# Earlier first tiles and a re-ordered output projection in a hybrid S5/Conformer step

## The chip, the cores and the metric

The kernel runs on one core of one Trainium2 chip. The core has a matrix engine (TensorE, PE in the profile, with its weight loads counted apart as PEld), a vector engine (VectorE, DVE), a scalar engine (ScalarE, ACT), a general engine (GpSimd, POOL) and a queue engine that here only issues transfers (SyncE, SP). 16 DMA engines move data. The metric is the device time of one execution in microseconds (us); less is better. The time before is 1400.62 us, the median of three runs from 1399.85 to 1401.19 us.

## The reference

One decoder layer is computed for 1024 prompt tokens and 8 sample tokens (1032 columns in all), model width 1024, in float32:

```python
xn = rmsnorm(x, g_mix);  z = xn @ w_in              # 1024 -> 3584
u, cv, cg = z[:, :512], z[:, 512:1024], z[:, 1024:1536]
gates = sigmoid(z[:, 1536:])                        # 2 x 1024
y, hr, hi = s5_layer(u, ...)                        # complex state scan, 32 groups x 64 states
yg = gelu(y) @ w_glu;  ya = yg[:, :1024] * sigmoid(yg[:, 1024:])
c = silu(layernorm(causal_dwconv(cv * sigmoid(cg))))   # 31 taps
yb = c @ w_pw
merged = gates[:, :1024] * ya + gates[:, 1024:] * yb
x = x + merged @ w_out
hn = rmsnorm(x, g_ffn) @ w_ff_in                    # 1024 -> 2 x 2816
x = x + (silu(hn[:, :2816]) * hn[:, 2816:]) @ w_ff_out
return rmsnorm(x, g_final), new states
```

## The kernel before, in words

Activations lie transposed: model channels on the 128 partitions, the 1032 tokens along the free axis. A product of float32 quality is made of three float16 products: each weight tile and each activation tile is split into a high half and a low half, and `mtile` (L584) or `mcol` (L1116) adds high x high, high x low and low x high in PSUM. So that the halves stay in range, every weight tile is first scaled by a power of two. `wload` (L565) is that chain for one 128-column slice of weights: `wdma` (L479) brings it as float32 into a tile `wr` (three buffers); `wscale` (L526) takes the sum of squares with one ScalarE instruction in `sumsq` (L513), then the maximum over partitions with GpSimd's partition_all_reduce in `spread` (L518), then two short VectorE steps in `pow2` (L497, L498); `wsplit16` (L556) writes the high half on ScalarE (L558) and the low half on VectorE (L562) into the tiles `wh` and `wl` (three buffers each). The squares themselves are of no use and are written into the tile that will later take the high half (`his[i].bitcast(BF16)`).

The stages are, in order: norm and transposes of the nine x tiles (`load_x`, `norm`, `xpose`, L647 to L723) together with the u columns of w_in (`u_chunk`, L733) and the parameters of the S5 branch (`prep`); the S5 scan (L839 on), with the convolution input `conv_in` and gate products as other work for TensorE; `glu` and the convolution; the pointwise product `pw` (L1092); the output projection `out` (L1132) with its weights `wout` (L1124); the FFN blocks (`ff_in` L1184, then w_ff_out); the final norm.

An identity matrix `ident` is needed for every transpose on TensorE. It is made by `make_identity` (L628), which ends in one GpSimd instruction, an affine select.

Around w_out: `residual(m)` (L1074) loads 128 channels of x again, transposes them in three PSUM tiles of pool `ms` (two banks, shared with other short uses) and copies them to `x1[m]` on ScalarE. All merged activations are then scaled by one number (`ascale`, from the maximum of `mss`) and split into `mh` for three token chunks. `out(c)` multiplies chunk c in groups of three, three and two columns of tiles, each group in a three-bank PSUM tile of pool `mm` (two such tiles), and adds the product, scaled by `io`, to `x1[m]` (L1143). `io` is made by one instruction (`invs`, L508) from `so`, which holds the scales of all eight w_out tiles.

The order of the work on each engine isn't written by hand. A planner simulates the program and takes, on each engine, the ready instruction of the highest priority; the priority is the place in the program, moved forward by 3000 places inside `hp()` and by 20000 inside `wscale`. On the chip each engine and each transfer queue then works strictly in the order fixed by the planner, and an instruction that waits holds up what is behind it. Tiles with a tag share a fixed number of buffers, and a tile waits until the last user of its buffer is done.

Of the kernel before, what the change touches and what calls it, by code (L numbers as in the profile page):

```python
# [9 lines left out]
F32 = mybir.dt.float32  # L10
# [8 lines left out]
P = 128  # L19
D = 1024  # L20
# [16 lines left out]
class S5:  # L37
# [400 lines left out]
def hybrid_step(ctx: ExitStack, tc: tile.TileContext, x_prompt, x_sample, state_ssm_re, state_ssm_im,  # L438
# [34 lines left out]
    def hp():  # L473
        return tc.high_priority(offset=HPO)
# [50 lines left out]

    def wscale(raws, his, o=None):  # L526
# [10 lines left out]
    def wscale_pe(raws, his):  # L537
        with tc.high_priority(offset=HPS):
            ss = cp.tile([P, 2], F32, name=nm("uss"), tag="uss", bufs=2)
            pt = pst.tile([P, 512], F32, name=nm("pws"), tag="pu")  # L540
            for i, raw in enumerate(raws):
                sumsq(raw, his[i].bitcast(BF16), ss[:, i:i + 1])
                T.matmul(pt[:, 0:1], ones, ss[:, i:i + 1], start=(i == 0), stop=(i == len(raws) - 1))
# [21 lines left out]
    def wload(src, r0, kt, c0):  # L565
        raw = wdma(src, r0, kt, c0)
        hi, lo = (wp.tile([P, kt, P], F16, name=nm(t), tag=t) for t in ("wh", "wl"))
        s = wscale([raw], [hi])
        return wsplit16(raw, hi, lo, s), s

    def wload2(src, cs, dst=None, o=None):
# [4 lines left out]
        h, l = dst or (wp.tile([P, 2, 4, P], F16, name=nm(t), tag=t) for t in ("wh", "wl"))  # L576
        s = wscale([raw], [h], o)
        wsplit16(raw, h, l, s)
# [93 lines left out]
    for r0, src, n in ((0, g_ffn, 8), (8, conv_b, 4), (12, conv_ln_g, 4), (16, conv_ln_b, 4)):  # L672
        GP.dma_start(gw[r0:r0 + n], src[0].rearrange("(r p) -> r p", p=P))
    pt = ms.tile([P, 512], F32, name="pgv", tag="ms")
# [83 lines left out]
    pairs = [wpair(), wpair()]  # L758
    wus = [wscale_pe(raw, [p[0] for p in pairs])]
# [314 lines left out]
    def residual(m):  # L1074
        xc = sb("xc", (P, 8, P))
        SY.dma_start(xc, x_prompt[0][:, m * P:(m + 1) * P].rearrange("(j k) d -> j k d", k=8))
        xcs = cp.tile([8, P], F32, name=nm("xcs"), tag="xcs", bufs=2)
        SY.dma_start(xcs, xsm[:, m * P:(m + 1) * P])
        x1[m] = xT = sa("x1")
        for q in range(3):  # L1080
            pt = ms.tile([P, 512], F32, name=nm("pxt"), tag="ms")
            if q < 2:
                for i in range(4):
                    T.transpose(pt[:, i * P:(i + 1) * P], xc[:, 4 * q + i], ident)
                A.copy(xT[:, 512 * q:512 * q + 512], pt)
            else:
                T.transpose(pt[:, :8], xcs, ident[:8, :8])
                A.copy(xT[:, D:], pt[:, :8])

# [42 lines left out]
    def out(c):  # L1132
# [48 lines left out]
    for c in range(3):  # L1181
        out(c)

    def ff_in(n, ss):  # L1184
        if n == 0:
            ws = [wload(w_ff_in, 0, 8, c0) for c0 in (0, DFF)]
            inv = [invs(s, gsc[:, 2:3]) for _, s in ws]
            pts = [mpsum() for _ in range(2)]
            for cs in ((0, 1), (2,)):
                for q in range(2):  # L1190
                    for c in cs:
                        a, b = B3[c], B3[c + 1]
                        mcol(ws[q][0], [(h[:, a:b], l[:, a:b]) for h, l in xg], pts[q][:, c, :b - a])
            g1, s1 = sa("g1"), sb("s1")
            with hp():
                for d, z, (a, b) in ((0, slice(0, 2), (0, 768)), (1, 2, (768, TOK))):
                    v = [t[:, a:b] if d else t[:, a:b].rearrange("p (c n) -> p c n", c=2) for t in (s1, g1)]
                    n_ = (b - a) if d else 384
                    A.activation(v[0], pts[0][:, z, :n_], AF.Sigmoid, scale=inv[0])
# [28 lines left out]
    def wlast(i):  # L1228
# [107 lines left out]
```

## Time and profile before

| what | value |
|---|---|
| median of 3 runs | 1400.62 us |
| profiled execution, its own time | 1400.05 us |
| its span in the trace | 1398.3 us |
| TensorE busy | 1303.8 us, 93% of the span |
| VectorE busy | 800.6 us, 57% |
| ScalarE busy | 535.3 us, 38% |
| GpSimd busy | 98.9 us, 7% |
| mean transfer rate | 69 GB/s |

TensorE is busy for all but 94.5 us of the span. The shares are means: between 710 and 1346 us, in the FFN, TensorE is busy without a break, while the idle time lies at the start, in the S5 stage, around w_out and at the end. A busy TensorE may also run at a lower granted clock (PEclk in the views of stretches, 1.00 is full speed).

### The profile page before, as it was taken

What the parts mean: (1) busy time and instruction counts of PE and PEld (TensorE: products, weight loads), DVE (VectorE), ACT (ScalarE), POOL (GpSimd) and SP (SyncE); (2) the same over time, 40 slices, a digit from 0 to 9 for tenths busy, and PEclk for the clock granted to TensorE, in tenths of its full rate; (3) what the DMA queues carried; (4) which work ended last, traced back from release to release, by engine and by line L of the source; (5) the groups of instructions that cost most, each with busy time, mean ns of one, the idle gap of its engine ahead of it and who ended that gap; (6) DMA issues with size and microseconds to landing.
All of it is one profiled execution on the core that took longest, in us unless ns stands there. A gap on an engine that the chain in (4) does not pass through costs nothing.

```text
span 1398.3 us, 22132 instructions
## 1 busy us (share of the span) xinstructions
PE 1303.8 (93%) x8877; PEld 892.6 (64%) x8877; DVE 800.6 (57%) x1830; ACT 535.3 (38%) x882; POOL 98.9 (7%) x208
## 2 busy tenths in 40 slices
PE   3898798999998999599989999999999999999996
PEld 2776565666665666367656666666666666666665
DVE  5976888989996635646532433335432434342547
ACT  5834333453334434822332422324232422342412
POOL 5000001100010000000000000000000000000100
PEclk9999899999998999799999999999999999999999
DMA  7445754341121115320011112111221112110103
GB/s 191 126 96 119 141 109 107 99 115 37 55 63 45 31 57 145 117 61 1 1 50 51 29 54 76 46 41 32 65 62 54 29 54 76 46 49 27 50 27 122
DMA packets 168976, 96.45 MB, mean 69 GB/s; under 512 B 12799, under 2 KB 165003, under 8 KB 168873
## 3 DMA queue, kind: packets, MB, share of 16 engines
q1 hardware_dynamic: 167469, 92.44, 24.3%
q0 software_dynamic: 896, 1.63, 0.6%
q8 instruction: 69, 1.13, 0.3%
q10 hardware_dynamic: 507, 0.97, 0.3%
q14 instruction: 35, 0.28, 0.1%
HBM read 76.72 MB, written 9.65 MB: 62 GB/s over the span
## 4 chain that ended last, share of the span: by engine, by line
PE 70%; DVE 14%; issue 9%; DMA 3%; ACT 1%; POOL 1%; SPq 1%; DVEq 0%; ACTq 0%; POOLq 0%
PE mm L591 57%; PE mm L1120 7%; DVE acc L895 3%; PE pfo L1278 2%; PE pu L731 2%; DVE wl L562 2%; DMA Y<-X 1%; DVE tb L895 1%; POOL sv L518 1%; DMA U<-ud 1%; DVE mg L968 1%; DMA M<-kvd 1%; DVE mg L965 0%; DVE xgt L1156 0%; PE ptr L721 0%
## 5 line engine op out<-in xcount | busy, mean ns | idle before, releaser
L591 PEld LDWEIGHTS <-wh 128*128 128x128 f16 x4656 | 457.5, 98 | 234.2 <-issue 5.4
L591 PE MATMUL mm<-xgp,wh 128*128 128x344 f16 x2016 | 350.6, 310 | 4.5 <-DVE py L497 4.5
L591 PEld LDWEIGHTS <-wl 128*128 128x128 f16 x2328 | 228.8, 98 | 112.3 <-issue 0.8
L513 ACT ACTIVATE wh<-wr 128x1024 bf16<-128x1024 f32 (+2 forms) x114 | 109.1, 957 | 407.0 <-PE mm L591 264.4
L591 PE MATMUL mm<-xn,wh 128*128 128x344 f16 (+2 forms) x1152 | 205.6, 313 | 1.9 <-ACT ut L743 1.1
L591 PE MATMUL mm<-xgp,wl 128*128 128x344 f16 x1008 | 202.7, 310 | 0.0
L562 DVE SCALAR_TENSOR_TENSOR wl<-wr,wsc,wh 128x1024 f16<-128x1024 f32 (+2 forms) x112 | 129.8, 1160 | 63.7 <-ACT wh L558 61.2
L558 ACT ACTIVATE wh<-wr,wsc 128x1024 f16<-128x1024 f32 (+2 forms) x112 | 117.0, 1045 | 116.5 <-DVE wsc L498 109.4
L591 PE MATMUL mm<-hp,wh 128*128 128x344 f16 x912 | 157.8, 309 | 0.0
L518 POOL PARTITION_ALL_REDUCE sv<-wss x124 | 67.1, 541 | 1088.6 <-ACT wh L513 1038.8
L523 DVE TENSOR_SCALAR sv<-sv 128x1 f32<-128x1 f32 x124 | 18.9, 152 | 180.7 <-POOL sv L518 180.7
L591 PE MATMUL mm<-xn,wl 128*128 128x344 f16 (+2 forms) x576 | 118.7, 313 | 0.0
L1210 DVE SCALAR_TENSOR_TENSOR g<-mm,inv,g 128x1032 f32<-128x1032 f32 x21 | 27.2, 1293 | 127.2 <-PE mm L591 127.2
L1120 PE MATMUL mm<-mh,wo 128*128 128x384 f16 (+1 forms) x576 | 90.3, 319 | 3.9 <-DVE x L1143 2.8
L591 PE MATMUL mm<-hp,wl 128*128 128x344 f16 x456 | 91.3, 309 | 0.0
L1261 DVE SCALAR_TENSOR_TENSOR x<-mm,inv,x 128x1032 f32<-128x1032 f32 x32 | 41.3, 1292 | 72.3 <-PE mm L591 72.3
L1120 PEld LDWEIGHTS <-wo 128*128 128x128 f16 x576 | 57.7, 101 | 35.3 <-issue 8.9
L591 PE MATMUL mm<-gyp,wh 128*128 128x344 f16 x384 | 66.6, 309 | 1.4 <-DVE mg L968 0.8
L895 DVE SCALAR_TENSOR_TENSOR acc<-t,cws,acc 128x511 f32<-128x511 f32 (+14 forms) x60 | 44.9, 749 | 0.0
L895 DVE SCALAR_TENSOR_TENSOR acc<-c,cw,acc 128x511 f32<-128x511 f32 (+14 forms) x60 | 43.6, 746 | 0.0
L591 PE MATMUL mm<-gyp,wl 128*128 128x344 f16 x192 | 38.4, 309 | 0.0
L1278 PE MATMUL pfo<-hp,wlp 128*128 128x392 f16 (+2 forms) x216 | 34.1, 309 | 0.0
(379 smaller groups left out, 1401.5 us busy)
## 6 DMA issues: line engine op xcount, KB each, us to landing
wr<-in_w_ff_in_dram SPq DMA_DIRECT2D x44, 512.0 KB
wr<-in_w_in_dram SPq DMA_DIRECT2D x28, 512.0 KB
wr<-in_w_ff_out_dram SPq DMA_DIRECT2D x24, 320.0 KB
xt<-in_x_prompt_dram SPq DMA_DIRECT2D x8, 512.0 KB
cosi<-pc SPq DMA_DIRECT2D x32, 128.0 KB
wr<-in_w_glu_dram SPq DMA_DIRECT2D x16, 256.0 KB
wr<-in_w_out_dram SPq DMA_DIRECT2D x8, 512.0 KB
xc<-in_x_prompt_dram SPq DMA_DIRECT2D x8, 512.0 KB
```

Source lines behind the costliest of these rows:

```text
L513: A.activation(junk, src, AF.Square, accum_out=o)
L518: GP.partition_all_reduce(v, ss, P, RMAX)
L523: V.tensor_scalar(v, v, 1e-28, None, MAXI)
L558: A.mul(hi, raw, s)
L562: V.scalar_tensor_tensor(lo[:, sl], raw[:, sl], s, hi[:, sl], MUL, SUB)
L591: T.matmul(pt[:, c, :b - a], ww[:, k], aa[:, a:b], start=(k == 0 and i == 0), stop=(k == n - 1 and i == 2))
L731: T.matmul(o, ww[:, k], aa[:, c0:c0 + w], start=(k == 0 and i == 0), stop=(k == 7 and i == 2))
L895: V.scalar_tensor_tensor(o[:, q:], x[:, 0:HT - q], w[q], o[:, q:], MUL, ADD)
L1120: T.matmul(o, w[a][:, k], acts[k][b], start=(k == 0 and i == 0), stop=(k == n - 1 and i == 2))
L1210: V.scalar_tensor_tensor(c3(g1), z, inv, c3(g1), MUL, MUL)
L1261: V.scalar_tensor_tensor(c3(x1[m]), z, inv, c3(x1[m]), MUL, ADD)
L1278: T.matmul(pt[:, :w], wl[m][a][:, k], hid[k][b][:, c0:c0 + w], start=(k == 0 and i == 0), stop=(k == nb - 1 and i == 2))
```

## The change

The change has four parts. The shortened diff:

```diff
-            dma.dma_start(t[64:128], t[0:64])
+            dma.dma_start(t[64:128], b[0].rearrange("g p c -> p g c"))
...
+    wjunk = cp.tile([P, D], BF16, name="wjunk")
-                sumsq(raw, his[i].bitcast(BF16), ss[:, i:i + 1])
+                sumsq(raw, jview(raw), ss[:, i:i + 1])
...
-    make_identity(nc, ident)
     GP.memset(zi[:, P:], 0.0)
-    GP.memset(ones, 1.0)
+    V.memset(ones, 1.0)
+    V.tensor_tensor_scan(jr, ones, ones, 0.0, MUL, ADD)
+    pj = ms.tile([P, 512], F32, name="pj", tag="ms")
+    T.matmul(pj[:, 0:1], jr[0:1, :], ones[0:1, 0:1], start=True, stop=True)
+    V.tensor_copy(jc, pj[:, 0:1])
+    V.tensor_scalar(ident, jr, jc, None, ALU.is_equal)
...
     s5.load_a(GP)
+    raw = [wdma(w_in, 0, 8, P * m) for m in range(2)]
     with hp():
         load_x(2)
-    raw = [wdma(w_in, 0, 8, P * m) for m in range(2)]
-    for k in range(3, NX):
-        load_x(k)
-    s5.load_b(GP)
+        load_x(3)
+    raw.append(wdma(w_in, 0, 8, 2 * P))
+    with hp():
+        for k in range(4, 9):
+            load_x(k)
+        s5.load_b(SY)
-    GP.dma_start(cwn, conv_w[0])
+    SY.dma_start(cwn, conv_w[0])
...
     def residual(m):
-        xc = sb("xc", (P, 8, P))
-        SY.dma_start(xc, ...)
+        with hp():
+            v = sb("xc", (P, 8, P))
+            SY.dma_start(v, ...)
-        for q in range(3):
-            pt = ms.tile([P, 512], F32, name=nm("pxt"), tag="ms")
...
+        pt = mpsum()
+        for q in range(2):
+            for i in range(4):
+                T.transpose(pt[:, q, i * P:(i + 1) * P], xc[q][:, i], ident)
+        T.transpose(pt[:, 2, :8], xcs, ident[:8, :8])
+        A.copy(xT[:, :512], pt[:, 0])
+        V.tensor_copy(xT[:, 512:D], pt[:, 1])
+        V.tensor_copy(xT[:, D:], pt[:, 2, :8])
...
         for gr in G3:                      # in out(c)
+            if c == 0:
+                for m in gr:
+                    if m >= 4:
+                        residual(m)
...
-    for m in range(3):
+    for m in range(6):
         wout(m)
     for m in range(4):
         residual(m)
...
-        for c in range(3):                 # all three chunks split under hp()
+    def msplit(c):                         # one chunk; hp() for chunk 0 only
+    msplit(0)
-    for m in range(3, 8):
+    for m in range(6, 8):
         wout(m)
-        if m < 7:
-            residual(m + 1)
     io = invs(so, mcx, "io", 1)
     for c in range(3):
+        if c < 2:
+            msplit(c + 1)
         out(c)
...
     def ff_in(n, ss):                      # n == 0
-        # products of chunks 0, 1 and of chunk 2 for both halves, then all gating under hp()
+        # products of chunks 0, 1, their gating at the priority of wscale; then chunk 2 likewise
```

First, the identity is made on VectorE (a running sum gives 1 to 128 along a row, one product on TensorE gives the same numbers down the partitions, one comparison gives the matrix). Second, the x tiles 2 to 8 are issued with high priority, and the S5 parameters of `load_b`, the convolution weights and the small vectors go through SP's queue instead of GpSimd's; both halves of B now come from HBM. Third, the squares of `wscale` and `wscale_pe` go to one scratch tile `wjunk`. Fourth, around w_out, six instead of three `wout` come ahead, residuals 4 to 7 move into `out(0)`, a residual uses one tile of pool `mm` and copies on two engines, the splits of chunks 1 and 2 come in between, and the gating of the first FFN tile is placed between its products.

More of the change, by code (lines that the diff above doesn't have):

```diff
@@ L6 @@
 from concourse import mybir
-from concourse.masks import make_identity
 from concourse._compat import with_exitstack
@@ L524, in spread, with jview, wscale @@
         return v
-    def wscale(raws, his, o=None):
+    wjunk = cp.tile([P, D], BF16, name="wjunk")
+    def jview(raw):
+        sh = list(raw.shape)[1:]
+        n = 1
+        for d in sh:
+            n *= d
+        j = wjunk[:, :n]
+        if len(sh) == 2:
+            return j.rearrange("p (a b) -> p a b", a=sh[0])
+        return j.rearrange("p (a b c) -> p a b c", a=sh[0], b=sh[1])
+    def wscale(raws, o=None):
         with tc.high_priority(offset=HPS):
@@ L535, in wscale, with wscale_pe @@
         return o
-    def wscale_pe(raws, his):
+    def wscale_pe(raws):
         with tc.high_priority(offset=HPS):
@@ L541, in wscale_pe @@
             for i, raw in enumerate(raws):
-                sumsq(raw, his[i].bitcast(BF16), ss[:, i:i + 1])
+                sumsq(raw, jview(raw), ss[:, i:i + 1])
                 T.matmul(pt[:, 0:1], ones, ss[:, i:i + 1], start=(i == 0), stop=(i == len(raws) - 1))
@@ L567, in wload @@
         hi, lo = (wp.tile([P, kt, P], F16, name=nm(t), tag=t) for t in ("wh", "wl"))
-        s = wscale([raw], [hi])
+        s = wscale([raw])
         return wsplit16(raw, hi, lo, s), s
@@ L576, in wload2 @@
         h, l = dst or (wp.tile([P, 2, 4, P], F16, name=nm(t), tag=t) for t in ("wh", "wl"))
-        s = wscale([raw], [h], o)
+        s = wscale([raw], o)
         wsplit16(raw, h, l, s)
@@ L627, in hybrid_step @@
     ident = zi[:, :P]
-    make_identity(nc, ident)
     GP.memset(zi[:, P:], 0.0)
     ones = cp.tile([P, P], F32, name="ones")
-    GP.memset(ones, 1.0)
+    V.memset(ones, 1.0)
+    jr = cp.tile([P, P], F32, name="jr")
+    V.tensor_tensor_scan(jr, ones, ones, 0.0, MUL, ADD)
+    pj = ms.tile([P, 512], F32, name="pj", tag="ms")
+    T.matmul(pj[:, 0:1], jr[0:1, :], ones[0:1, 0:1], start=True, stop=True)
+    jc = cp.tile([P, 1], F32, name="jc")
+    V.tensor_copy(jc, pj[:, 0:1])
+    V.tensor_scalar(ident, jr, jc, None, ALU.is_equal)
     e5, e5c, e5t, est = ExitStack(), ExitStack(), ExitStack(), ExitStack()
@@ L663, in hybrid_step @@
     s5.load_a(GP)
+    raw = [wdma(w_in, 0, 8, P * m) for m in range(2)]
     with hp():
         load_x(2)
-    raw = [wdma(w_in, 0, 8, P * m) for m in range(2)]
-    for k in range(3, NX):
-        load_x(k)
-    s5.load_b(GP)
+        load_x(3)
[4 more added lines that the diff above has]
+        s5.load_b(SY)
     cwn = kp.tile([CW, 512], F32, name="cwn", tag="Q", bufs=2)
-    GP.dma_start(cwn, conv_w[0])
+    SY.dma_start(cwn, conv_w[0])
     for r0, src, n in ((0, g_ffn, 8), (8, conv_b, 4), (12, conv_ln_g, 4), (16, conv_ln_b, 4)):
-        GP.dma_start(gw[r0:r0 + n], src[0].rearrange("(r p) -> r p", p=P))
+        SY.dma_start(gw[r0:r0 + n], src[0].rearrange("(r p) -> r p", p=P))
     pt = ms.tile([P, 512], F32, name="pgv", tag="ms")
@@ L758, in hybrid_step @@
     pairs = [wpair(), wpair()]
-    wus = [wscale_pe(raw, [p[0] for p in pairs])]
+    wus = [wscale_pe(raw[:2])]
     wui = [invs(wus[0], gxc[:, 1:2], "uinv", 2)]
@@ L763, in hybrid_step @@
     wu.append(wsplit16(raw[1], *pairs[1], wus[0], parts=4))
-    raw += [wdma(w_in, 0, 8, P * m) for m in range(2, 4)]
-    for k in range(NX, 9):
-        load_x(k)
+    raw.append(wdma(w_in, 0, 8, 3 * P))
     norm(groups[1])
@@ L769, in hybrid_step @@
     pairs = [[kt_(t, bufs=2) for _ in range(2)] for t in ("cosi", "M")]
-    wus.append(wscale_pe(raw[2:4], [p[0] for p in pairs]))
+    wus.append(wscale_pe(raw[2:4]))
     wui.append(invs(wus[1], gxc[:, 1:2], "uinv", 2))
@@ L1074, in residual @@
     def residual(m):
-        xc = sb("xc", (P, 8, P))
-        SY.dma_start(xc, x_prompt[0][:, m * P:(m + 1) * P].rearrange("(j k) d -> j k d", k=8))
+        with hp():
+            v = sb("xc", (P, 8, P))
+            SY.dma_start(v, x_prompt[0][:, m * P:(m + 1) * P].rearrange("(j k) d -> j k d", k=8))
+        xc = [v[:, 0:4], v[:, 4:8]]
         xcs = cp.tile([8, P], F32, name=nm("xcs"), tag="xcs", bufs=2)
@@ L1079, in residual @@
         x1[m] = xT = sa("x1")
-        for q in range(3):
-            pt = ms.tile([P, 512], F32, name=nm("pxt"), tag="ms")
[L1082 to L1088, printed above, removed]
+        pt = mpsum()
[6 more added lines that the diff above has]
+        V.tensor_copy(xT[:, D:], pt[:, 2, :8])
     wpw, mss = [], cp.tile([P, 8], F32, name="mss")
@@ L1126, in wout @@
         t = pair(sa("wo", (P, 2, 8, P), F16))
-        s = wscale([raw], [t[0]], so[:, m:m + 1])
+        s = wscale([raw], so[:, m:m + 1])
         wo.append(wsplit16(raw, t[0], t[1], s))
@@ L1170, in hybrid_step @@
         msc, mcx = ascale(mss, "msc")
-        for c in range(3):
+    def msplit(c):
+        with tc.high_priority(offset=HPO if c == 0 else 0):
             for m in range(8):
@@ L1188, in ff_in @@
             pts = [mpsum() for _ in range(2)]
-            for cs in ((0, 1), (2,)):
+            g1, s1 = sa("g1"), sb("s1")
+            for z, c0, c1 in ((slice(0, 2), 0, 2), (2, 2, 3)):
                 for q in range(2):
-                    for c in cs:
+                    for c in range(c0, c1):
                         a, b = B3[c], B3[c + 1]
                         mcol(ws[q][0], [(h[:, a:b], l[:, a:b]) for h, l in xg], pts[q][:, c, :b - a])
[L1194 to L1198, printed above, removed]
+                a, b = B3[c0], B3[c1]
+                n_ = 384 if c0 == 0 else b - a
+                v = [t[:, a:b].rearrange("p (c n) -> p c n", c=2) if c0 == 0 else t[:, a:b] for t in (s1, g1)]
+                with tc.high_priority(offset=HPS):
                     A.activation(v[0], pts[0][:, z, :n_], AF.Sigmoid, scale=inv[0])
@@ L1233, in wlast @@
         h, l = pair(sa("wlp", (P, 2, nb, 2 * P), F16))
-        s = wscale([raw], [h], swl[:, i:i + 1])
+        s = wscale([raw], swl[:, i:i + 1])
         wsplit16(raw, h, l, s)
@@ L1302 @@
 NA = 21
-NX = 5
 GA = 5
```

## The prediction

> **What bounds the kernel now.** I read the page, then a table of stretches, then the timeline at the stretches where TensorE (PE) isn't full. Columns of the table: stretch, its length, busy us of PE, PEld, DVE, ACT, POOL, then PE's granted clock, DMA share, GB/s.
>
> ```profile
> span 1398.3 us, 22132 instructions
> 0.00:14.00 14.00, 0.02 (x1) 0.02 (x1) 0.27 (x1) 4.73 (x7) 1.90 (x10) 1.00 0.92 257
> 14.00:18.00 4.00, 1.35 (x5) 1.16 (x5) 3.22 (x28) 2.19 (x4) 3.99 (x6) 1.00 0.63 228
> 18.00:24.00 6.00, 4.43 (x16) 2.76 (x16) 5.61 (x38) 3.33 (x7) 6.00 (x8) 1.00 0.55 117
> 24.00:34.00 10.00, 6.26 (x39) 5.26 (x38) 9.95 (x49) 7.47 (x15) 6.70 (x19) 1.00 0.50 125
> 34.00:54.00 20.00, 15.07 (x115) 11.93 (x115) 18.81 (x97) 17.59 (x34) 0.97 (x2) 0.91 0.54 169
> 54.00:84.00 30.00, 29.80 (x260) 25.77 (x261) 28.07 (x104) 17.55 (x34) 0.00 (x0) 1.00 0.23 63
> 240.00:437.00 197.00, 191.42 (x1297) 128.28 (x1294) 185.78 (x338) 83.36 (x111) 20.50 (x23) 0.99 0.26 72
> 553.90:626.70 72.80, 56.83 (x322) 34.37 (x321) 39.18 (x84) 42.26 (x82) 3.21 (x9) 0.88 0.35 102
> 704.00:710.00 6.00, 6.00 (x28) 3.30 (x26) 2.71 (x5) 2.20 (x3) 0.00 (x0) 0.61 0.31 91
> 710.00:1346.00 636.00, 636.00 (x4364) 426.74 (x4362) 246.62 (x492) 214.18 (x310) 31.33 (x80) 1.00 0.17 50
> ```
>
> From 710 to 1346 PE is busy in every microsecond at full clock: nothing in the change shortens that, however soon weights are ready. The same holds nearly for 240 to 437. The change can gain in three places: 0 to 54 (PE idle 14 + 2.65 + 1.57 + 3.74 + 4.93 = 26.9), around w_out (554 to 627) and at the entry of the FFN (699 to 710).
>
> **Part 1, identity and first transfers.** Timeline of the start:
>
> ```profile
> 4.89 1.06 ACT L702 ACTIVATE junk<-xt 128x1024 bf16<-128x1024 f32 x1 [2.24 <-DMA xt<-in_x_prompt_dram]
> 13.64 0.28 POOL masks.py:199 TENSOR_SCALAR_AFFINE_SELECT zi<-zi 128x128 f32<-128x128 f32 x1 [11.44 <-issue]
> 14.29 0.17 DVE L677 COPY gt<-pgv 128x8 f32<-128x8 f32 x1 [10.88 <-PE pgv L675]
> 17.41 0.75 DVE L707 TENSOR_SCALAR xt<-xt,ry 128x1024 f32<-128x1024 f32 x1
> 26.89 0.15 PEld L731 LDWEIGHTS <-wh 128*128 128x128 f16 x1
> 28.84 3.27 SPq L482 DMA_DIRECT2D wr<-in_w_in_dram  x2
> 34.30 1.06 ACT L513 ACTIVATE wu<-wr 128x1024 bf16<-128x1024 f32 x1 [2.79 <-DMA wr<-in_w_in_dram]
> masks.py:199 POOLq MODIFY_POOL_CONFIG  x2: 37/37/37, 2.3 to 2.3; - x2
> 93.09 1.03 PE L591 MATMUL mm<-xn,wh 128*128 128x344 f16 x6 [1.12 <-ACT ut L743]
> L518 POOLq MODIFY_POOL_CONFIG  x2: 1/1/1, 31.2 to 31.3; - x2
> 38.15 0.38 POOL L518 PARTITION_ALL_REDUCE sv<-wss  x1 [7.11 <-ACT wh L513]
> L371 DVE TENSOR_TENSOR_SCAN Y<-mag,X x32: 393/398/424, 121.9 to 245.8; 128x128 f32<-128x128 f32 x32
> ```
>
> GpSimd changes its configuration at 2.3 us and reaches the affine select only at 13.64; until then PE and DVE stand still, though the first x tile was squared at 4.89. The new identity needs a memset, a scan (0.40, the L371 row), one small product with its hand-overs (0.37, which lies between the end of the affine select and the copy at 14.29), a copy (0.17, as L677) and a 128x128 comparison (no row; between that 0.17 and the 0.75 of eight times its size, L707, I take 0.3, nearer to its own size). Two more hand-overs at 0.2 make it 1.3 to 2.1 us, so with a start in the first 1 or 2 us, as nothing is waited for, it is ready at about 3, ahead of the first squares (4.89 + 1.06 = 5.95). The identity then costs the path nothing; without that cover it costs 2 us.
>
> What is late next? The weights: the second w_in tile and the scales it needs. At the 257 GB/s of the first row, the four tiles x0, x1 and two of w_in (2.1 MB) take 8.2 us and land by about 10. From the squares to the first u product I allow 3 us, so about 14 against 26.89: 13 earlier. But DVE is nearly full from then on: 3.22 + 5.61 + 9.95 + 18.81 + 28.07 = 65.7 us busy in the 70 from 14 to 84. It can now begin at about 6 with the norm of x0. That is 8 earlier, and DVE sets the stage, so I take 8. Bounds: 12 (most of PE's 26.9 idle, less the 14 that first transfers and weights still need), and -3, a loss, if what now stands in SP's queue costs more than it brings (next).
>
> The x tiles 5 to 8 stood behind two weight transfers in SP's queue that waited for a free `wr` (28.84, 3.27 long); now they go ahead. In their place 17 short transfers stand ahead of w_in tile 3, which was squared at 34.30 and of which half of the u products depend. Their rows, by median time to landing on POOL's queue:
>
> ```profile
> cn<-in_ssm_c_im_dram POOLq DMA_DIRECT2D x2, 128.0 KB, 2.7
> B<-in_ssm_b_im_dram POOLq DMA_DIRECT2D x1, 128.0 KB, 5.7
> h0n<-in_state_ssm_re_dram POOLq DMA_DIRECT2D x2, 64.0 KB, 3.8
> ```
>
> Landing includes latency that overlaps. From below they cost their bytes, 1.3 MB at 257 GB/s, 5 us; from above all in a row: 4 x 2.7 + 4 x 5.7 + 3 x 3.8 and six small ones at about 3, 63 us. I take 15, nearer to the lower end, since the transfers of the first row, at 257 GB/s, can't each have paid a latency either. All x tiles and three of weights (4.2 + 1.6 MB) land by about 24 at that rate, tile 3 then at about 39, 5 later than before. Until then PE has the first half of the u products: 192 of 384, at 29.80 / 260 = 0.115 of the 54:84 row 22 us, and the transposes beside them, from 14 to about 40. So I count nothing.
>
> The trace has the configuration change a second time, ahead of the first all-reduce (31.2 to 38.15), hidden in POOL's idle time. With the affine select gone it stays, at most as long as the 11.44 above, and the weights behind it are those of the convolution, which PE first used at 93.09. By the Trainium skill (GPSIMD Engine Reference, 2.1 Instruction dispatch) the first call to a freshly loaded GpSimd kernel pays about 6 us with no instruction in the profile. The trace shows up to 11.3 us for the first case and at most 6.9 for the second, so the rule agrees in kind; by its figure the identity would have cost 6 and part 1 would gain about 3 instead of 8.
>
> **Part 2, scratch tile.** No instruction is added. ScalarE no longer needs a free `wh` for the squares:
>
> ```profile
> L513 ACT ACTIVATE wh<-wr 128x1024 bf16<-128x1024 f32 (+2 forms) x114 | 109.1, 957 | 407.0 <-PE mm L591 264.4
> ```
>
> Those 264 us of waits lie under a full PE, so by themselves they are worth nothing. Successive squares overwrite one tile on the same engine, in order, so no wait is added. I take 0 in the middle of the kernel, with -4 to +4 for a plan that comes out otherwise. It counts in parts 3 and 4.
>
> **Part 3, w_out.** From the last pointwise product:
>
> ```profile
> 553.92 1.04 PE L1084 MATMUL pxt<-zi,xc 128*128 128x128 f32 x8
> 564.73 0.22 PE L1087 MATMUL pxt<-zi,xcs 8*128 8x8 f32 x1 [3.70 <-ACT x L1085]
> 565.90 5.27 PE L1120 MATMUL mm<-mh,wo 128*128 128x384 f16 x23 [0.20 <-DVE mh L606]
> 564.99 10.46 SPq L1078 DMA_DIRECT2D xcs<-in_x_sample_dram  x2
> 575.74 4.16 SPq L482 DMA_DIRECT2D wr<-in_w_out_dram  x2
> 591.75 0.23 DVE L508 TENSOR_SCALAR inv<-so,asc 128x8 int32<-128x8 int32 x1
> 592.76 34.09 PE L1120 MATMUL mm<-mh,wo 128*128 128x384 f16 x199 [2.77 <-DVE x L1143]
> 627.27 6.66 PE L1120 MATMUL mm<-mh,wo 128*128 128x384 f16 x40
> 559.85 4.37 ACT L605 ACTIVATE mh<-mg,asc 128x384 f16<-128x384 f32 x9
> L1085 ACT COPY x<-pxt x16: 564/585/607, 554.6 to 592.1; 128x512 f32<-128x512 f32 x16
> ```
>
> No product can leave PSUM before `inv` at 591.75, because it needs the scale of the eighth w_out tile, and the last w_out transfers stood behind an SP wait of 10.46 us for `xcs`. Meanwhile PE also waited for copies of x queued behind the splits on ScalarE (3.70). Work at full clock in the 72.8 us: 1 + 23 + 2 + 22 + 199 = 247 products at 6.66 / 40 = 0.167, 41 us, and eight transposed tiles at 1.3, 10: 51. So 22 are lost. After: the scale of `mg` is still due at about 559.5, with four residuals (5.2) under it: 1 lost. Then the first chunk's splits (0.49 each) feed PE at its own pace. Six w_out tiles are done earlier and the last two need only `wr` and scratch, so `inv` is no longer awaited. The added waits: residuals 4 to 7 take `mm` tiles between the groups, and what follows on PE waits for two copies of 0.585 on two engines, some 1 us each, 4; lower clock after gaps, 3. 22 - 8 = 14. Bounds: 19, and 4 if the PSUM tiles or ScalarE (42.26 busy of 72.8) hold it up.
>
> **Part 4, entry of the FFN.**
>
> ```profile
> 698.80 1.06 ACT L513 ACTIVATE wh<-wr 128x1024 bf16<-128x1024 f32 x1 [2.17 <-PE mm L1120]
> 703.01 0.48 DVE L1200 SCALAR_TENSOR_TENSOR g<-mm,inv,s 128x264 f32<-128x264 f32 x1
> 703.55 1.90 PE L591 MATMUL mm<-xgp,wh 128*128 128x344 f16 x6 [4.50 <-DVE py L497]
> ```
>
> PE stops at 698.9 with both `mm` tiles full; their gating stands on ScalarE behind squares that waited for the last product, and PE goes on just when L1200 ends (703.49), for 6 us at clock 0.61 (2.3 lost). With the squares in scratch and the gating of chunks 0 and 1 during the products of chunk 2, 4.5 + 2.3 = 6.8 are at stake; about 1.3 of gating may stay (the 0.48 of L1200 for 264 columns, and its like on ScalarE and for the other 768). I take 5.5, bounds 0 and 7. By the Trainium skill (TensorE: Matmul & The Clock Gate, What's actually happening) a cold array runs at half clock for about 3.4 us, which would make 1.7 instead of 2.3 and the sum 0.6 less.
>
> **Sum.** 8 + 0 + 14 + 5.5 = 27.5. The profiled execution took 1400.05, its span and 1.75 around it, 0.57 under the median. 1400.05 - 27.5 + 0.57 = 1373.1: I say 1373.
>
> **Rivals.** (a) The start's gain is lost again in the S5 stage, where chains of transfers and VectorE wait on one another and the plan is new: 19.5 remain, 1381. For it: DVE is busy 185.8 of 197 from 240 to 437. Against: PE's gaps before that come from the chain, which also starts earlier. (b) Part 3 gives only its 4, because residuals and groups share two PSUM tiles: 17.5, 1383. For it: those copies stood in PE's way before (3.70). (c) All parts at their upper bounds, 38: 1363. (d) Slower: the parameter transfers jam SP's queue. Place: ahead of w_in tile 3. In a row and with short runs at twice their landing time they cost 63 + 23 for B's four, so tile 3 lands at 24 + 86 = 110. From its landing, 30 us more (22 for 192 u products, about 6 for squares, scale and halves at 1.06 to 1.3 each, 2 of gaps) end the stage at 140 against 93: +47, less 19.5, so 1428. It decides from a landing at about 82. Against: B's landing of 5.7 already holds its short runs. That short runs are slow is stated by the Trainium skill too (DMA: Bandwidth & Descriptors, Specifications: below 512 B no line rate); no row here has B on SP's queue. (e) The change doesn't do what it says: the planner places x tiles behind weights anyway; then part 1 still has its identity, and it falls into (a).
>
> **How the numbers follow.** Forecast 0.55 (its own range 1362 to 1385), (a) with (e) 0.15, (b) 0.12, (c) 0.10, (d) 0.08. This kernel's measurement tells about 0.2%, 2.8 us, from no change. Faster takes all but the weakest 0.03 of (a) and (d): 0.89; same 0.03 + 0.01 of (d): 0.04; slower 0.07. The range 1360 to 1392 leaves out (d) and the tails.
>
> **What would show it.** Right: first transpose of x before 11 (its scaling stood at 17.41), first u product before 17; `inv` of w_out no later than the first group's end; 554 to 627's work in under 62 us; no stop over 2 us at L591 after the last L1120; full PE through the FFN as before. Wrong: PE idle on w_in tile 3 after 40, new gaps at `pxt`, or an S5 stage longer than before by as much as the start is shorter.

## The result and the profile after

The changed kernel took 1413.04 us (median of 5 runs, 1406.17 to 1414.84) against 1400.62 for the kernel before beside it (1398.38 to 1403.04): a ratio of 1.0079, with a 95% interval of 1.0051 to 1.0106. It is slower, by 12 us of the medians and 11 by the ratio. Ratios leave out the slow runs, of which there were two: one of the kernel before beside gate, late_wo, no2_ldt and no2_ga6 (1432.77) and one of only1 (1973.30). I had forecast 1373. Neither the forecast nor any of the five rivals holds: the place that I had priced at nothing, part 2, lost more than the other parts gained.

From the page of the changed kernel, its span and the groups of the weight squares, of the scales behind them on VectorE and of the high halves:

```profile
span 1413.1 us, 22055 instructions
L512 ACT ACTIVATE wjunk<-wr 128x1024 bf16<-128x1024 f32 (+3 forms) x128 | 123.2, 963 | 443.7 <-DMA wr<-in_w_ff_in_dram 183.1
L522 DVE TENSOR_SCALAR sv<-sv 128x1 f32<-128x1 f32 x124 | 18.9, 152 | 345.7 <-POOL sv L517 343.3
L569 ACT ACTIVATE wh<-wr,wsc 128x1024 f16<-128x1024 f32 (+2 forms) x112 | 116.9, 1044 | 131.2 <-PE mm L602 122.4
```

The first group answers to the row `L513 ... x114 | 109.1, 957 | 407.0 <-PE mm L591 264.4` of before. One square takes as long as it did (963 ns, 957 before). What it waits for has changed: then a product (a free `wh`), now a transfer (its own `wr`), and the wait for a product has moved to the high half itself (L569). The same shows in the list of ScalarE's waits between 60 and 600 us (total us, how often, longest). Before:

```profile
ACT wh L558 <- DVE wsc L498: 71.6, 21, 12.5
ACT wh L513 <- issue: 27.9, 7, 7.0
ACT gb L513 <- DVE mg L1098: 22.2, 6, 4.8
ACT wh L513 <- PE mm L591: 21.7, 11, 6.3
```

and after (a row of 16.0 us of another kind is left out before the last):

```profile
ACT wjunk L512 <- DMA wr<-in_w_in_dram: 85.5, 18, 13.7
ACT ysg L982 <- PE mm L602: 26.9, 7, 4.5
ACT wjunk L512 <- DMA wr<-in_w_glu_dram: 24.7, 7, 7.8
ACT wh L569 <- PE mm L602: 21.1, 17, 3.5
ACT wjunk L512 <- DMA wr<-in_w_out_dram: 18.3, 7, 7.1
ACT wjunk L512 <- DMA wr<-in_w_pw_dram: 15.1, 4, 5.3
```

ScalarE now stands 144 us (85.5 + 24.7 + 18.3 + 15.1) before squares whose tile has not landed, and everything behind them in its queue stands too. Where that hurts is seen in stretches of the trace (length, busy us of PE, PEld, DVE, ACT, POOL, then PE's granted clock, DMA share, GB/s). Before, from 290 to 330:

```profile
290.00:330.00 40.00, 38.84 (x267) 25.91 (x266) 36.37 (x72) 20.56 (x26) 3.20 (x6) 1.00 0.22 65
```

and after, at that place, in the start and in the FFN:

```profile
0.00:14.00 14.00, 3.29 (x12) 2.46 (x12) 6.89 (x51) 7.03 (x11) 5.49 (x19) 1.00 0.91 271
14.00:34.00 20.00, 13.92 (x83) 10.15 (x83) 18.50 (x108) 19.07 (x36) 0.24 (x1) 1.00 0.87 206
34.00:54.00 20.00, 16.56 (x108) 12.25 (x108) 17.79 (x94) 14.40 (x30) 1.33 (x4) 0.74 0.42 122
290.00:330.00 40.00, 29.75 (x172) 18.64 (x171) 29.07 (x60) 15.66 (x20) 1.43 (x4) 0.83 0.16 46
725.00:1340.00 615.00, 611.47 (x4190) 409.72 (x4189) 230.60 (x460) 204.33 (x295) 30.57 (x74) 1.00 0.17 49
```

PE, full from 290 to 330 before but for 1.2 us, now idles 10 and has less clock for the rest; in the FFN, where it had been full in every microsecond, it loses 3.5.

To follow the loss through all the kernels I summed each trace's products by the columns that they stream. The table gives how many us later (+) or earlier (-) than in the kernel before the same amount of that work is reached. It is good to about 1 us, at 560 to about 2. Its columns are named in the experiments.

```
before at  after   no2 only1 only2 only34  gate only2_gate late_wo no2_ga6
   20       -6.6  -6.4  -6.3  -0.2   0.8   -6.8    0.3      -6.4    -5.4
   40       -9.5  -9.1  -9.2   0.3   1.0   -8.7    0.2      -8.8    -8.3
   60       -2.3  -2.1  -1.3   6.8   0.7   -4.4   -1.3      -1.9    -2.0
  300       -3.6  -5.8  -4.2  22.7  -1.8  -17.0    0.0      -5.3    -4.6
  320       11.2  -0.1   1.9  30.9  -0.4   -8.0    2.4      -3.2    -5.3
  440       13.2  -0.7   1.3  30.7  -0.8  -10.3    2.3      -1.3    -3.2
  560       23.1  -0.1   1.8  32.4   1.0   -7.6    3.0       4.4    -3.7
  600       13.1 -10.4   1.5  28.3  -7.8  -14.1    2.7      -7.6   -13.7
  680       13.4 -10.2   1.5  28.6  -7.7  -13.8    2.7      -6.9   -12.8
  720       10.3 -15.8   3.6  31.3 -11.8  -17.7    0.7      -8.0   -18.0
 1340       14.6 -15.8   3.6  39.2 -11.8  -17.5    0.7      -4.1   -18.0
```

In the first column the start is 9.5 ahead at 40 and gives most of it back by 60; the w_out stage (560 to 600) gains 10 and the FFN's entry (680 to 720) 3, as hoped; and 15 go at the first w_glu block (300 to 320), 10 in the pointwise stage (440 to 560) and 4 in the FFN.

### The profile page after: what moved, and what is told of

It reads as the page before. It is cut to its first block, busy times and chain, and to the rows that moved or that the text cites. A ratio compares the mean times of both kernels' runs of the same rounds, so it can differ in the third digit from the quotient of the medians.

```text
span 1413.1 us, 22055 instructions
## 1 busy us (share of the span) xinstructions
PE 1307.5 (93%) x8879; PEld 895.1 (63%) x8879; DVE 798.8 (57%) x1850; ACT 528.8 (37%) x866; POOL 74.9 (5%) x188
## 4 chain that ended last, share of the span: by engine, by line
PE 41%; issue 25%; DVE 7%; POOL 2%; ACT 1%; DMA 1%; ACTq 0%; POOLq 0%; DVEq 0%; SPq 0%
PE mm L602 32%; PE mm L1139 6%; PE pfo L1305 2%; POOL sv L517 2%; DVE hp L617 1%; DVE wl L573 1%; DVE acc L913 1%; DVE mh L617 1%; DMA wr<-in_w_ff_out_dram 1%; PE mm L1103 1%; DVE tb L913 1%; ACT wh L569 0%; DVE xgt L1179 0%; PE tr L1314 0%; ACT wjunk L512 0%
## 5 line engine op out<-in xcount | busy, mean ns | idle before, releaser
L512 ACT ACTIVATE wjunk<-wr 128x1024 bf16<-128x1024 f32 (+3 forms) x128 | 123.2, 963 | 443.7 <-DMA wr<-in_w_ff_in_dram 183.1
L522 DVE TENSOR_SCALAR sv<-sv 128x1 f32<-128x1 f32 x124 | 18.9, 152 | 345.7 <-POOL sv L517 343.3
L602 PE MATMUL mm<-xn,wh 128*128 128x344 f16 (+2 forms) x1152 | 202.6, 310 | 4.4 <-ACT ut L763 2.4
L569 ACT ACTIVATE wh<-wr,wsc 128x1024 f16<-128x1024 f32 (+2 forms) x112 | 116.9, 1044 | 131.2 <-PE mm L602 122.4
L517 POOL PARTITION_ALL_REDUCE sv<-wss x124 | 56.6, 456 | 1093.6 <-ACT wjunk L512 1059.6
L602 PE MATMUL mm<-gyp,wh 128*128 128x344 f16 x384 | 70.3, 320 | 10.2 <-ACT gyp L616 5.0
L602 PE MATMUL mm<-chp,wh 128*128 128x344 f16 x192 | 33.2, 309 | 3.9 <-ACT gb L1088 2.0
```

What stands on the lines that cost most here:

```text
L512: A.activation(junk, src, AF.Square, accum_out=o)
L517: GP.partition_all_reduce(v, ss, P, RMAX)
L522: V.tensor_scalar(v, v, 1e-28, None, MAXI)
L569: A.mul(hi, raw, s)
L602: T.matmul(pt[:, c, :b - a], ww[:, k], aa[:, a:b], start=(k == 0 and i == 0), stop=(k == n - 1 and i == 2))
```

## The experiments

Each is compared with the kernel before on the same chip. Its median there was between 1395.95 and 1399.59, so ratios say more than differences from 1400.

**Part 2 taken back, and part 2 alone.** "no2" is the changed kernel with the old target of the squares, "only2" the kernel before with the scratch tile and nothing else. The edit of no2, shortened; only2 has it the other way round:

```diff
-                sumsq(raw, jview(raw), ss[:, i:i + 1])
+                sumsq(raw, his[i].bitcast(BF16), ss[:, i:i + 1])
```

> The changed kernel with part 2 undone: the squares go into the weight's own high half again, as before; parts 1, 3 and 4 stay. Theory A (the scratch tile is what costs: free of the wait for `wh`, squares are placed in ScalarE's queue ahead of weights that have not landed, and what stands behind them is late): the stop of about 13 us between 300 and 320, at the start of the w_glu products, is gone, and so are the 4 us of gaps in the FFN; with the start's 3, w_out's 6 and the entry's 2.5 kept, 1385 to 1396. Theory B (the new order of the first transfers makes a plan in which PE has used up its other products before the w_glu weights come): the stop between 300 and 320 stays, 1408 to 1416.

> The kernel before with part 2 alone: squares into the scratch tile. Theory A: slower, 1408 to 1418, with the stop at the first w_glu products and small gaps later. Theory B: within 3 us of before, 1398 to 1403, with no such stop. My prediction put this at 0, with 4 us either way.

Measured: no2 1389.53 (ratio 0.9944, 0.9922 to 0.9966), only2 1438.56 (1.0286, 1.0252 to 1.0321). Both fall on theory A's side, and only2 far beyond its range. So part 2 turns a kernel that is 0.6% faster into one that is 0.8% slower, and alone costs 40 us by its ratio. In its column of the table this comes in pieces: 6.8 by 60, 16 more by 300, 8 by 320 and 8 in the FFN.

How it comes about shows at the first w_glu block of the changed kernel (start, length, engine, line, out<-in, and in brackets what ended the wait):

```profile
268.65 1.06 ACT L512 ACTIVATE wjunk<-wr 128x1024 bf16<-128x1024 f32 x1 [7.23 <-DMA wr<-in_w_in_dram]
270.63 0.40 SPq L422 DMA_DIRECT2D out_dram<-so  x1
274.37 0.93 SPq L586 DMA_DIRECT2D wr<-in_w_glu_dram  x2
276.37 2.44 SPq L843 DMA_DIRECT2D gd<-gy  x4
279.61 1.06 ACT L512 ACTIVATE wjunk<-wr 128x1024 bf16<-128x1024 f32 x1 [6.39 <-DMA wr<-in_w_glu_dram]
294.15 0.38 POOL L517 PARTITION_ALL_REDUCE sv<-gss  x1 [12.93 <-ACT gyp L512]
304.70 4.29 ACT L616 ACTIVATE gyp<-gyt,asc 128x1032 f16<-128x1032 f32 x4 [1.71 <-DVE asc L497]
305.91 1.02 PE L602 MATMUL mm<-gyp,wh 128*128 128x344 f16 x3 [5.04 <-ACT gyp L616]
314.07 1.06 ACT L512 ACTIVATE wjunk<-wr 128x1024 bf16<-128x1024 f32 x1 [5.08 <-DMA wr<-in_w_glu_dram]
317.32 1.88 PE L602 MATMUL mm<-gyp,wh 128*128 128x344 f16 x6 [4.13 <-ACT mg L973]
```

and the same in no2:

```profile
266.12 0.39 SPq L422 DMA_DIRECT2D out_dram<-so  x1
266.61 1.84 SPq L831 DMA_DIRECT2D gd<-gy  x3
285.43 0.38 POOL L517 PARTITION_ALL_REDUCE sv<-gss  x1 [3.24 <-ACT gyp L512]
296.95 4.29 ACT L604 ACTIVATE gyp<-gyt,asc 128x1032 f16<-128x1032 f32 x4 [3.06 <-DVE asc L497]
302.19 1.10 ACT L961 ACTIVATE mg<-mm,inv 128x1032 f32<-128x1032 f32 x1
303.34 1.61 PE L590 MATMUL mm<-gyp,wh 128*128 128x344 f16 x6 [4.65 <-ACT mg L961]
```

In the changed kernel ScalarE waits 7.23 and 6.39 us for weights that landed only then. The store of `so` goes out 4.5 us later than in no2. ScalarE's last step on `gy` (the scan's output) comes at 272.56, in no2 at 263.91, and its last stores leave at 276.37, behind a w_glu transfer in SP's queue. `gyp` is the pair of halves that w_glu multiplies; the reduction over `gss`, which sets its scale, comes 8.7 later (294.15 against 285.43). The last square ahead of that reduction also waits 2.50 us for the transfer of `scn`, which ScalarE's own queue issued behind the late square, at 283.72, in no2 at 275.74. Then PE stops for `gyp`, and again for a copy of gate products from PSUM to `mg` behind one more late square.

**Is it the wait, or the tile?** "gate" keeps the scratch tile and puts only the lost wait back, in the changed kernel; "only2_gate" does so where part 2 stands alone.

```diff
+    def gated(raw, hi, o):
+        one = hi[(slice(None),) + (0,) * (len(hi.shape) - 2) + (slice(0, 2),)].bitcast(F32)
+        A.copy(one, ones[:, 0:1])
...
+            A.activation(jview(raw), raw, AF.Square, scale=one, accum_out=o)
...
-                sumsq(raw, jview(raw), ss[:, i:i + 1])
+                gated(raw, his[i], ss[:, i:i + 1])
```

> The changed kernel, scratch tile and all, but each weight square waits for a free high half again: ScalarE first copies a 1.0 into two columns of it, and the square takes that 1.0 as its scale. The squares still go to the scratch tile. In the order of ScalarE's program a square then stands a median of 2 instructions ahead of its tile's split, as without part 2; with the scratch tile alone it was 7. Theory A1 (the lost wait moves the squares too far ahead in ScalarE's queue): most of what part 2 costs comes back, at 0.2 us more ScalarE per tile: 1386 to 1397. Theory A2 (the tile itself, or anything else in part 2): 1402 to 1415.

> The kernel before with part 2 alone, each weight square made to wait for a free high half again by a 1.0 copied into it. Part 2 alone took 1438.6. Theory A1 (the lost wait is what costs): back to the time before within 6 us, 1391 to 1403. If part 2 alone loses by something else as well: 1408 to 1430.

Measured: gate 1385.80 (0.9913, 0.9891 to 0.9934), only2_gate 1401.81 (1.0013, 1.0003 to 1.0022). Theory A1 holds in both, though gate lies 0.2 below its range: with one more ScalarE instruction for each weight square, 38 us of part 2's 40 come back (by the ratios), and in the whole change all of it. The distance between a tile's square and its split in ScalarE's order, in instructions, over the 128 tiles:

```
               median  mean
before            2     3.4
no2               2     3.7
after             7    11.9
only2             7    12.6
gate              2     3.7
only2_gate        2     3.4
```

In gate, ScalarE's list of waits between 60 and 600 is headed by the wait for the high half again, and the first wait for a raw weight stands twelfth (7.6 us in all, for w_out):

```profile
ACT wh L516 <- PE mm L608: 51.9, 16, 7.4
ACT wh L575 <- DVE wsc L497: 49.7, 18, 9.3
```

So the cause is the lost wait. Which of the queues loses most isn't settled. VectorE's wait for the reduction behind the square doubled too (L522 above: 343.3, before 180.7), and the two weren't tried apart; late_wo below has a stop that runs through both.

**A lower priority** ("after_pri") was meant to move the squares back in another way.

```diff
     def wscale(raws, o=None):
-        with tc.high_priority(offset=HPS):
+        with tc.high_priority(offset=HPO):
```

> The changed kernel with the scratch tile kept, but the squares and scales of weights planned at the ordinary raised priority (3000) in place of 20000. Theory A1 (it is the place of the squares in the engines' queues: with no `wh` to wait for, the raised priority puts them ahead of work that is ready): the stop of 10 us at the first w_glu products and the smaller ones in the LayerNorm, pointwise and FFN stages go, 1385 to 1397. Theory A2 (the tile itself, or `wr` transfers that start at other times, costs, wherever the squares stand): 1402 to 1415, with the stop at w_glu still there.

Measured: 1410.79 (1.0080, 1.0055 to 1.0105). Read as written this speaks for A2, but ScalarE's program came out the same, instruction by instruction: the priority changed nothing, and so the run tells nothing. Of the two ways tried, only the dependency held the squares back.

**The scratch tile from w_out on** ("late_wo").

```diff
-                sumsq(raw, jview(raw), ss[:, i:i + 1])
+                sumsq(raw, jview(raw) if late else his[i].bitcast(BF16), ss[:, i:i + 1])
...
+    late.append(1)
     for m in range(6):
         wout(m)
```

> The changed kernel with the scratch tile used from w_out on only; the weights before it are squared into their high halves. Theory A1: no stop at the first w_glu products and none at the LayerNorm and pointwise products; what is left of the loss is the FFN's 4 us against the kernel without part 2 (1389.5): 1391 to 1396. If parts 3 and 4 need the scratch tile to give what they give: 1380 to 1387. If part 2's loss is set in the whole by one stage after w_out: over 1400.

Measured: 1397.09 (0.9991, 0.9976 to 1.0005), just above the first range. As expected the stop at the first w_glu block is mild, and the FFN loses 4. But 5.7 more go between 440 and 560. In the trace that is one stop of PE of 5.86 us, until 562.51: a square of a w_ff_in tile (558.76) waits 3.42 us for its transfer, VectorE stands 5.03 for the reduction behind that square, and the copies out of the PSUM tile that PE needs are queued behind VectorE's step. And the FFN's entry gives 1.1 instead of no2's 5.6. From 440 to 720 late_wo gains 6.7 and no2 15.1: parts 3 and 4 don't need the scratch tile, and are worth more without it.

**Part 1 alone, and parts 3 and 4 alone** ("only1", "only34"): the hunks of the diff as they stand, on the kernel before.

> The kernel before with part 1 alone: identity without GpSimd, x tiles first, parameters on SP's queue. Theory A: the start is 3 us shorter and nothing is lost later, 1396 to 1399. Theory B: a stop of over 8 us at the first w_glu products, 1405 to 1414. My prediction put this part at 8 us, 1392.

> The kernel before with parts 3 and 4 alone: residuals around w_out and the gating at the FFN's entry, with squares still into the high half. If these parts gain what the changed kernel shows (6 and 2.4), 1390 to 1394; if they can gain only with the scratch tile (the squares of w_out and w_ff_in wait for a free tile again), 1398 to 1402; by my prediction's 14 + 5.5, 1381.

Measured: only1 1402.25 (1.0029, 1.0009 to 1.0049), only34 1388.16 (0.9937, 0.9922 to 0.9952). Parts 3 and 4 give their gain without the scratch tile, somewhat more than I had expected by then: 8.8 between 560 and 600 and 4.1 at the entry. Part 1 gives nothing, and its column shows where: 9.2 ahead at 40, 1.3 at 60; 4.2 at 300, 1.9 behind at 320.

**Why the start's gain goes.** Four kernels. "p1gp" is part 1 with the parameter transfers on GpSimd's queue, "no2gp" the same in no2, "ident34" has the new identity and parts 3 and 4 but the old transfers, "no2_ldt" is no2 with the log_dt transfer first on ScalarE's queue. The edit of the first two, shortened:

```diff
-        s5.load_b(SY)
+        s5.load_b(GP)
-    SY.dma_start(cwn, conv_w[0])
+    GP.dma_start(cwn, conv_w[0])
...
```

> The kernel before with part 1, but the parameter transfers (load_b, conv_w and the four gains) left on GpSimd's queue. In part 1 alone PE was 9 us ahead at 40 and only 1 at 60, as the second half of the first u products waited for w_in tile 3 (squared at 35.9, before 34.3) and its scale. Theory C (tile 3 behind the parameter transfers is what gives the start's gain back): tile 3 is squared before 26, PE is 5 to 9 us ahead at 60, and 1390 to 1397 in the end. Theory D (VectorE, full from 14 on, gives it back, or the transfers and VectorE of the S5 stage do): within 3 us of part 1 alone, 1397 to 1404, whenever tile 3 lands.

> The changed kernel without part 2 and with the parameter transfers on GpSimd's queue. Theory C: 4 to 8 us below the same kernel with them on SP's queue (1389.5), 1381 to 1386. Theory D: 1386 to 1392.

> The kernel before with the new identity and parts 3 and 4; the transfers' order and queues as before, squares into the high half. Theory D (what the start gains is lost by the S5 stage): as parts 3 and 4 alone, 1385 to 1391. If the identity alone brings the start forward and it stays: 1379 to 1384.

> The changed kernel without part 2, with the log_dt transfer issued first on ScalarE's queue instead of GpSimd's. VectorE stood 5.75 us at the head of its queue for that transfer, with the gain's maximum and the norm of x0 behind it. If that wait holds the start: the first x transpose comes at 9 to 10 instead of 12.7. By theory D the end moves by under 2 us, 1388 to 1391; if the start's time is carried to the end, 1385 to 1387.

Measured: p1gp 1401.57 (1.0019, 1.0010 to 1.0029), no2gp 1389.32 (0.9935, 0.9920 to 0.9950), ident34 1390.34 (0.9947, 0.9927 to 0.9966), no2_ldt 1394.26 (0.9971, 0.9957 to 0.9985). The first three times are those of theory D: however the start is arranged, none of it reaches the end. Where it is lost differs. The reduction over `gss` starts at 291.89 before, at 287.45 in only1 and 285.43 in no2, but at 297.89 in p1gp, 296.03 in no2gp, 294.96 in ident34 and 300.35 in no2_ldt. So in only1 and no2 the S5 stage hands on 4 to 6 us of the lead, and they are lost behind it; in the other four they are gone before. And p1gp doesn't refute theory C as I meant it to. Its tile 3 didn't come before 26:

```profile
27.53 1.96 SPq L481 DMA_DIRECT2D wr<-in_w_in_dram  x2
40.27 0.14 DVE L497 TENSOR_SCALAR usc<-py 128x1 int32<-128x1 int32 x1
```

With SP's queue cleared its transfer goes out at 27.53, 0.1 after the first of three `wr` is free. In only1 that `wr` was free at 23.86 and the transfer went out at 31.98: there SP's queue held it for 8 us. But in p1gp the parameter transfers on GpSimd's queue delayed the second w_in tile (squared at 20.03, in only1 at 12.66), and so `wr` came free 3.6 later. One delay stands in for the other, and the scale of the second half comes at 40.27 against 42.73, a shift of 2.5 us. What tile 3 would give with neither delay stays open. In no2_ldt the wait just became another one:

```profile
7.01 0.18 DVE L52 TENSOR_SCALAR ex_x<-ldt 128x32 f32<-128x32 f32 x1 [4.39 <-DMA ldt<-in_ssm_log_dt_dram]
12.28 0.88 PE L729 MATMUL ptr<-zi,xt 128*128 128x128 f32 x3
```

The first transpose came 0.4 earlier than in no2 (12.70), not 3, and the end about 4 later by the ratios; my expectation there failed on both counts. From 14 to 34 its PE is busy 6.92 us, in no2 14.64, with one wait of 9.4 us for VectorE ahead of a product of the S5 preparation; why the plan comes out so I haven't followed.

**The second place where it goes** is the wait of 4.65 us for the copy to `mg` in no2's rows above, behind four splits. `GA` is the number of gate blocks (w_in's products for `gates`, each copied to an `mg`) ahead of the first w_glu block. "no2_ga6" has six, which puts that copy ahead of the splits; "only34_ga6" has six where no such wait stands; "gate_ga6" joins both corrections.

```diff
-GA = 5
+GA = 6
```

> The changed kernel without part 2, with six gate blocks (GA) in place of five ahead of the first w_glu block. Without part 2 PE was 6 us ahead at 300 and level at 310: it waited 4.65 us for a PSUM tile, whose copy to `mg` stood in ScalarE's queue behind the four splits of gyp and a weight square. With six blocks that copy stands ahead of the splits, as it does before the change. Theory E (this place in the queue takes what the start gained): 1382 to 1386. Theory D (the S5 stage's transfers set the first w_glu product, whatever ScalarE's order): 1388 to 1391.

> The kernel before with parts 3 and 4 and with six gate blocks (GA) in place of five. Here the copy to `mg` stands ahead of the four splits of gyp with five blocks already, and PE waited under 2 us at the first w_glu block. Theory E: there is no stop to take away, so as with five blocks, within 2.5 us of 1388 (1386 to 1390.5). If six gate blocks help whatever the start: 1381 to 1384.

> The changed kernel with the wait for a free high half put back and six gate blocks. The wait alone gave 1385.8, six blocks without the scratch tile 1383.0. If both corrections add: 1377 to 1382. With the wait put back, the copy to `mg` may stand ahead of the splits already; then six blocks bring nothing: 1383 to 1388.

Measured: no2_ga6 1382.98 (0.9892, 0.9875 to 0.9909), only34_ga6 1389.05 (0.9922, 0.9904 to 0.9941), gate_ga6 1386.06 (0.9914, 0.9889 to 0.9940). In no2_ga6:

```profile
293.92 1.10 ACT L961 ACTIVATE mg<-mm,inv 128x1032 f32<-128x1032 f32 x1
294.92 4.28 ACT L604 ACTIVATE gyp<-gyt,asc 128x1032 f16<-128x1032 f32 x4
310.26 1.04 PE L590 MATMUL mm<-gyp,wh 128*128 128x344 f16 x6
```

The copy stands ahead of the splits, and PE reaches `gyp` without a wait. Its column keeps the 5 us at 320. Where no such wait stood, six blocks brought nothing. So theory E holds. Nor do six blocks bring anything in gate_ga6, which falls in its second range: in gate the copy stands ahead of the splits already. Gate's PE is 17.0 ahead at 300 and 8.0 at 320, as it there waits 4.89 us for `gyp`, whose reduction comes no sooner (285.21) than no2's. The lowest ratio here is no2_ga6's, 1.1% under the kernel before and 1.9% under the changed one; its interval overlaps those of gate and gate_ga6.

## Why the prediction was wrong, step by step

**Part 2 is the step that failed.** I wrote "Those 264 us of waits lie under a full PE, so by themselves they are worth nothing", and "no wait is added". The first stands; the second fails. The wait for a free `wh` did a second thing: it kept the planner from placing a square before its time. With it gone the squares came 7 instead of 2 instructions ahead of their split, and each took up ScalarE until its transfer landed. A wait was added after all, not to the square's operands but to everything queued behind it. I gave it 0 with 4 either way; it is worth 40 alone (by the ratio) and, between no2 and the changed kernel, 19 by the ratios (1.0079 / 0.9944 = 1.0136 of 1390) and 30 by the two profiled runs, no2's being the shortest of its four. I asked what is queued behind a waiting instruction for SP (rival d) and not for ScalarE.

**Part 1.** The new identity came as worked out, ready at about 2.6; the first transpose didn't make the "before 11", since VectorE stood first in line for the log_dt transfer (in p1gp, where that wait doesn't stand ahead of the norm, it came at 8.64). The first u product came at 21.03 instead of "before 17", against 27.10 before:

```profile
2.33 0.29 DVE L648 TENSOR_SCALAR zi<-jr,jc 128x128 f32<-128x128 f32 x1
8.31 0.18 DVE L52 TENSOR_SCALAR ex_x<-ldt 128x32 f32<-128x32 f32 x1 [5.13 <-DMA ldt<-in_ssm_log_dt_dram]
12.46 0.90 PE L741 MATMUL ptr<-zi,xt 128*128 128x128 f32 x3 [1.35 <-DVE xt L727]
21.88 1.66 DVE L573 SCALAR_TENSOR_TENSOR wl<-wr,usc,wh 128x256 f16<-128x256 f32 x4
31.13 2.93 SPq L481 DMA_DIRECT2D wr<-in_w_in_dram  x2
35.24 1.06 ACT L512 ACTIVATE wjunk<-wr 128x1024 bf16<-128x1024 f32 x1 [1.03 <-DMA wr<-in_w_in_dram]
41.99 0.14 DVE L497 TENSOR_SCALAR usc<-py 128x1 int32<-128x1 int32 x1
```

Tile 3 of w_in was squared at 35.24, sooner than my 39, so rival (d) is out. SP's queue did hold it, though: the `wr` that it needed was free at 23.54 (21.88 + 1.66) and its transfer went out at 31.13, behind the short transfers, which took that queue from 13.56 to 30.31, 17 us against the 15 I took. I had set that against the cover and counted nothing, and I had counted to the landing of the tile and not to its scale. The cover I had named, the first half of the u products until 40, was too thin: the second half's scale came at 41.99, nearly 7 us after the square started, and from 34 to 54 PE is busy 16.56 of 20 at a granted clock of 0.74 (before 15.07 at 0.91); the 0.74 is a mean of 0.50 from 36 to 44 and 1.00 from 46 on. The 8 us that I booked were there at 40 (9.5) and not at 60 (2.3). I had argued that VectorE sets the stage and starts 8 earlier, so all moves by 8. VectorE did get ahead: by 54 it had worked 43 us (6.89 + 18.50 + 17.79) against 38 (0.27 + 3.22 + 5.61 + 9.95 + 18.81). That PE had little of it at 60 because the lead went into the preparation of the S5 stage is argued and not shown. What was left by 300 went behind the splits, which is rival (a) with another mechanism than the one I gave it; that much no2_ga6 shows. Part 1 is worth between nothing (no2 against only34, 0.9944 and 0.9937) and a loss of 4 us (only1, 1.0029) instead of +8; with GA = 6 it is worth 4 (no2_ga6 against only34_ga6, 0.9892 and 0.9922, whose intervals just overlap).

**Part 3.** The mechanism was right and the size off: 8.8 to 10.3 instead of 14 (560 to 600: only34, no2, and 10.0 in the changed kernel; 6.5 in gate and 12.0 in late_wo), within its bounds; the stage of 72.8 us comes to about 63, just over my mark of 62. `inv` came ahead of the first product, as forecast:

```profile
579.16 1.97 PE L1103 MATMUL mm<-zi,xc 128*128 128x128 f32 x8 [4.57 <-DVE gb L1116]
586.54 0.22 DVE L507 TENSOR_SCALAR inv<-so,asc 128x8 int32<-128x8 int32 x1
588.83 0.48 PE L1139 MATMUL mm<-mh,wo 128*128 128x384 f16 x1 [3.40 <-ACT mh L616]
```

The term that was mis-sized in the changed kernel is the "1 lost" before the first product: the residuals waited 4.57 us for a PSUM tile of the last pointwise block, and the first product 3.40 more for a half of `mg`. By that alone 22 - (4.57 + 3.40 + 4 + 3) = 7 would be left; as 10.0 came, the 4 and the 3 that I allowed for later copies and clock were too much there. Part of the 4.57 is part 2's doing, as VectorE stands for a weight's scale (1.91) and high half (1.02) just ahead of the read that frees that tile. In no2 the waits ahead of the first product sum to 3.6, and two later ones for VectorE's sums into `x1` to 4.0. Rival (b), only 4, is out.

**Part 4** was right in kind and within its bounds: 5.6 in no2, 4.1 in only34 and 3.1 in the changed kernel (680 to 720) against 5.5. In the changed kernel the stop at the entry is 2.06 us, just over my mark of 2:

```profile
715.96 0.49 DVE L1227 SCALAR_TENSOR_TENSOR g<-mm,inv,s 128x264 f32<-128x264 f32 x1
716.50 1.05 PE L602 MATMUL mm<-xgp,wh 128*128 128x344 f16 x6 [2.06 <-DVE g L1227]
```

**"Nothing in the change shortens the FFN"** was right, but I didn't ask what might lengthen it. Full for 615 us before, PE waited four times for the scale of the hidden values (total, times, longest):

```profile
PE mm L602 <- DVE py L496: 3.5, 4, 1.1
```

Sum of the terms without part 2, by no2's column: 0 + 10.3 + 5.6 = 15.9 of the 27.5; by its ratio 8 us. The two differ mostly because the profiled run of before was a long one (1400.05, against a median of 1395.95 beside no2) and no2's a short one. In rival (c) I added the upper bounds of parts 1, 3 and 4 to 38 and left out the 4 of part 2; with it they make 42.

## What to carry to other kernels

A wait on a buffer is also what holds an instruction back in the order that a planner writes. Before you take one away, ask where the instruction will stand then, what it waits for there (a transfer, as a rule), and what is queued behind it on the same engine; if it should stay late, give it a dependency, as a lower priority may change nothing. A head start is worth only what the next stage can take: follow it from stage to stage to the end before you book it.

## What the runs showed of the hardware

Transfers with short runs hold the DMA engines as long as big ones while they move little. From 14 to 18 us both of these stretches show all 16 DMA engines taken. In p1gp, with the transfers of B and other parameters from GpSimd's queue under way (348 packets with 0.45 MB):

```profile
14.00:18.00 4.00, 0.69 (x2) 0.29 (x2) 1.65 (x11) 0.20 (x1) 1.65 (x3) 1.00 1.04 113
```

and in the changed kernel, with x tiles for the most part (454 packets with 1.67 MB):

```profile
14.00:18.00 4.00, 2.75 (x11) 1.90 (x11) 3.96 (x34) 3.46 (x8) 0.00 (x0) 1.00 1.03 417
```

The share is the same at 113 and at 417 GB/s. The changed kernel shows it too, with B on SP's queue: a share of 0.92 at 92 GB/s from 24 to 26. I had priced these transfers by a rate of 257 and by their landings one after the other. Neither counts what they take from other transfers at the same time: with nothing but their queue changed, the second w_in tile was squared at 20.03 in p1gp and at 12.66 in only1.
